# Hybrid decoder step: S5 tables by outer products, reversed S5 input at evacuation, first norm from token-major x, split weights kept as parts

## The chip, the cores and the metric

One Trainium2 chip, one of its cores. The metric is the device time of one execution of the program in microseconds (us). The engines have their own instruction queues, each worked off in order: TensorE (PE: matmuls; PEld: weight loads), VectorE (DVE), ScalarE (ACT), GpSimd (POOL) and SyncE (SP), which computes nothing and issues every DMA of this kernel.

## What is computed

One layer of a decoder trunk for 2048 prompt tokens and 8 sample tokens, width 1024, all in float32. Cut to its frame:

```python
z = rmsnorm(x, norm_mix) @ w_in                       # 2584 columns: mLSTM, S5 and gated-DeltaNet inputs
mix = concat([mlstm(z), s5(z) * glu, gated_delta_net(z)])
x = x + mix @ w_out
x = x + softmax(rmsnorm(x) @ w_mq @ mk.T / 16) @ mv @ w_mo    # 4 heads, 256 memory tokens
h = rmsnorm(x); x = x + (silu(h @ w_gate) * (h @ w_up)) @ w_down
y = rmsnorm(x)
```

S5 is a complex diagonal recurrence in 32 channel groups of 64 states: h[t] = lam * h[t-1] + B u[t], y[t] = Re(C h[t]) + d u[t]. The kernel runs it in chunks of 8 tokens, and for that needs tables made from lam: B times the powers 0 to 7 of lam, C times the powers 1 to 8, and the unit-size powers 0 to 128 of lam^8 (the array E).

## The kernel before

**Split matmuls.** Every float32 product is made of three fp32r matmuls. `gemm3` multiplies wh with xh, wh with xl and wl with xh: h is the value rounded to fp32r, l the rest. `split_x` and `hsplit` split activations (tiles H, ACT and DVE). Weights are split as they arrive, in `w_split_`: a DMA brings a raw tile wr of 128 x 1024 (512 KB), ACT rounds it to wh, and a subtraction gives wl:

```python
        S.copy(wh[:, 0:n], raw[:, 0:n])
        TT(V if i < 2 or i > 360 else G, wl[:, 0:n], raw[:, 0:n], wh[:, 0:n].bitcast(F32), SUB)
```

That is on GpSimd (G) for weights 2 to 360 of 512 and on VectorE (V) for the rest. wr, wh and wl have three buffers each. `load_w` runs two weights ahead with splits and up to three more with raw tiles. One weight serves 24 matmuls of 512 columns.

**Stages.** The prompt is cut into four segments of 512 tokens; the 8 sample tokens ride along. `win` does the input projection of a segment: 18 weights, one feature tile each, whose PSUM results (P) are scaled by the norm's row factors R and written out by DVE in `evac` (tile t), and then three token-major weights. The first `win` is interleaved with 16 tiles of memory keys and values (`mem_tile`), the next two with `fold` (products of those with attention weights). After the four `win` come four `post`, one for each segment, each over the same 95 weights: GLU, output projection, attention, FFN (22 gate, 22 up, 24 down); in segments 0 and 1 eight more for the sample tokens. So each of the 95 is fetched and split four times.

**Background work.** `s5_tables` (during the first `win`), `gdn`, `mlstm`, `s5` and the sample group's work are generators; `tick` moves them on by fixed rates between the weights' matmuls, and `drain` finishes what is left at fixed points (`s5_tables` after the first `win`). A scheduler then orders the instructions of each engine. `s5_tables` works with big tiles (three buffers, tag big), makes powers of lam by repeated complex products (`cmul`, six DVE instructions each), and writes tables to DRAM (T1, TB) from where transposes at L1166 and the S5 steps read them.

**First norm.** `win_sq` squares the feature-major x tiles on ACT and adds them up on DVE (`sq_acc`, tile acc); `norm_a` transposes acc on TensorE (L351) and reduces.

Of the kernel before, what the change touches and what calls it, by code (L numbers as in the profile page):

```python
# [66 lines left out]
def build(ctx, tc, I, O):  # L67
# [886 lines left out]
    def s5_tables():  # L954
        A0, A1 = Arena(), Arena()
        AB = Arena(bt())
        LN, RG = slice(0, 16), slice(16, 48)
# [107 lines left out]
        pb = [A0(bq), A0(bq)]  # L1065
        for q0 in (0, 8):
# [4 lines left out]
            Br = br[:, 0:1024].rearrange("p (q s c) -> p q s c", q=8, s=8)  # L1071
            Bi = bi[:, 0:1024].rearrange("p (q s c) -> p q s c", q=8, s=8)
            cmul(Br[:, :, 0, :], Bi[:, :, 0, :], bcq(cr, q0), bcq(ci, q0), pb[0], pb[1], tb[0], tb[1])
            for s_ in range(1, 8):
# [1159 lines left out]
```

## Time and profile before

| | |
|---|---|
| median of 3 runs | 3303.79 us (3300.41 to 3306.91) |
| the profiled execution, its own time | 3299.76 us, span 3298.0 us |
| TensorE busy | 3063.1 us, 93% of the span |
| VectorE busy | 2337.6 us, 71% |
| ScalarE, GpSimd busy | 1114.5 us (34%), 1103.8 us (33%) |
| DMA queue of SyncE | 448.43 MB, 45.7% of 16 engines' span |
| mean granted TensorE clock | 0.966 |

Times in the profile count from the start of the span. "Busy" is the time in which an engine executes; idle time before an instruction is put down to what ended it. The granted clock is 1 at TensorE's upper level and 0.5 at its lower. DMA share is the mean busy share of the 16 DMA engines. A helper's line stands for all its callers: L152 is any tensor-tensor instruction, L155 any scalar-tensor-tensor, L164 any matmul, so a tile's name tells which.

### The profile page before, as it was taken

The page shows a single profiled execution, that of the slowest core. Times are in us where ns is not written, and L with a number is a line of the kernel's source. Part 1 is how long each engine was busy: PE and PEld are TensorE (multiplying, and loading weights), DVE is VectorE, ACT ScalarE, POOL GpSimd, SP SyncE. Part 2 cuts the span into 40 slices and gives each one's busy share as a digit, 9 for nine tenths or more (in the row PEclk, how much of TensorE's full clock was granted, in tenths as well). Part 3 has the DMA queues.
Part 4 walks back from the last instruction along what each step waited for, and adds up shares of the span by engine and source line. Part 5 has one row for each costly group of instructions (what it writes and reads, how often), then busy time and mean ns, then how long its engine had stood idle before and what let it go on. Part 6 is the DMA issues. An engine that isn't in the chain of part 4 may idle for free.

```text
span 3298.0 us, 49267 instructions
## 1 busy us (share of the span) xinstructions
PE 3063.1 (93%) x18202; PEld 2619.2 (79%) x18202; DVE 2337.6 (71%) x4746; ACT 1114.5 (34%) x1882; POOL 1103.8 (33%) x706
## 2 busy tenths in 40 slices
PE   7777889999888998998999999989999999999998
PEld 6676678778877776787789999978777877888886
DVE  8783695786788689668886787687766767554445
ACT  3123433422542332234432322244324224332222
POOL 6332545534354444444544444344411000000000
PEclk9887999999999999999999999999999999999999
DMA  6679666666445345335443444352333325222332
GB/s 208 176 183 206 205 184 212 200 193 173 144 129 182 90 122 166 103 111 168 144 121 117 125 124 125 100 164 84 105 94 108 104 90 182 88 91 95 96 90 77
DMA packets 361361, 451.58 MB, mean 137 GB/s; under 512 B 144820, under 2 KB 246556, under 8 KB 361120
## 3 DMA queue, kind: packets, MB, share of 16 engines
q1 hardware_dynamic: 361120, 448.43, 45.7%
q8 instruction: 144, 2.36, 0.3%
q14 instruction: 97, 0.79, 0.1%
HBM read 378.73 MB, written 71.73 MB: 137 GB/s over the span
## 4 chain that ended last, share of the span: by engine, by line
PE 61%; DVE 13%; issue 3%; ACT 2%; DMA 2%; SPq 0%; POOL 0%; DVEq 0%; POOLq 0%; ACTq 0%
PE P L164 54%; PE M L164 5%; DVE t L155 3%; DVE big L152 3%; DVE x L152 1%; DVE s5h L155 1%; DVE TB L155 1%; DVE acc L152 1%; ACT wh L292 1%; DMA t<-mixd 1%; DVE x L155 1%; DVE H L152 0%; DVE H L155 0%; DMA x<-in_xT 0%; DMA ABd<-AW 0%
## 5 line engine op out<-in xcount | busy, mean ns | idle before, releaser
L164 PE MATMUL P<-H,wh 128*128 128x512 f32 (+2 forms) x8032 | 2190.0, 360 | 80.1 <-DVE t L152 32.7
L164 PEld LDWEIGHTS P<-H,wh 128*128 128x128 f32 x8032 | 1419.4, 191 | 309.4 <-issue 30.9
L164 PE MATMUL P<-H,wl 128*128 128x512 f32 (+2 forms) x4016 | 1430.8, 357 | 13.8 <-POOL wl L152 13.8
L152 POOL TENSOR_TENSOR wl<-wr,wh 128x1024 fp32r<-128x1024 f32 (+2 forms) x359 | 863.5, 2409 | 970.4 <-ACT wh L292 861.7
L292 ACT CAST wh<-wr 128x1024 fp32r<-128x1024 f32 (+3 forms) x512 | 521.1, 1020 | 1198.1 <-PE P L164 705.1
L164 PEld LDWEIGHTS P<-H,wl 128*128 128x128 f32 x4016 | 766.9, 191 | 124.6 <-POOL wl L152 16.3
L152 DVE TENSOR_TENSOR x<-x,P 128x512 f32<-128x512 f32 (+2 forms) x312 | 181.2, 587 | 141.9 <-PE P L164 128.9
L152 DVE TENSOR_TENSOR big<-big,big 32x87 f32<-32x87 f32 (+16 forms) x500 | 249.6, 499 | 18.7 <-DMA big<-ABd 10.8
L164 PE MATMUL P<-wh,H 128*128 128x256 f32 (+1 forms) x1280 | 244.6, 289 | 8.2 <-ACT pp L1717 6.3
L152 DVE TENSOR_TENSOR t<-P,R 128x512 f32<-128x512 f32 (+2 forms) x190 | 109.6, 581 | 165.7 <-PE P L164 142.0
L152 POOL TENSOR_TENSOR rs<-rcol,mhalf 128x4 f32<-128x4 f32 (+2 forms) x17 | 20.7, 1218 | 598.5 <-DVE rcol L161 598.2
L164 PEld LDWEIGHTS P<-wh,H 128*128 128x128 f32 x1280 | 204.7, 193 | 12.0 <-ACT pp L1717 8.2
L152 DVE TENSOR_TENSOR wl<-wr,wh 128x1024 fp32r<-128x1024 f32 (+1 forms) x153 | 183.8, 1202 | 25.5 <-ACT wh L292 22.8
L164 PE MATMUL P<-wl,H 128*128 128x256 f32 (+1 forms) x640 | 183.0, 287 | 0.5 <-POOL wl L152 0.5
L155 DVE SCALAR_TENSOR_TENSOR t<-P,R 128x512 f32<-128x512 f32 (+1 forms) x120 | 69.6, 583 | 153.9 <-PE P L164 152.2
L155 DVE SCALAR_TENSOR_TENSOR t<-t,t 128x512 f32<-128x512 f32 (+3 forms) x140 | 146.7, 1052 | 37.5 <-ACT t L1830 23.2
L152 DVE TENSOR_TENSOR H<-t,H 128x512 fp32r<-128x512 f32 (+1 forms) x120 | 123.5, 1037 | 46.3 <-ACT H L1600 46.2
L164 PEld LDWEIGHTS P<-wl,H 128*128 128x128 f32 x640 | 123.6, 193 | 1.2 <-POOL wl L152 0.7
L1600 ACT CAST H<-t 128x512 fp32r<-128x512 f32 (+1 forms) x120 | 73.5, 621 | 141.7 <-DVE t L152 124.8
L155 DVE SCALAR_TENSOR_TENSOR t<-g,VEC,t 128x256 f32<-128x256 f32 x144 | 99.5, 691 | 20.0 <-ACT t L724 18.4
L155 DVE SCALAR_TENSOR_TENSOR H<-x,VEC,H 128x512 fp32r<-128x512 f32 (+2 forms) x104 | 102.2, 996 | 8.5 <-ACT H L334 6.6
L152 DVE TENSOR_TENSOR acc<-acc,t 128x512 f32<-128x512 f32 (+1 forms) x115 | 99.1, 861 | 9.2 <-ACT t L343 7.3
(414 smaller groups left out, 3114.7 us busy)
## 6 DMA issues: line engine op xcount, KB each, us to landing
wr<-in_wgate SPq DMA_DIRECT2D x88, 512.0 KB
...
```

Source lines behind the costliest of these rows:

```text
L152: eng.tensor_tensor(out=out, in0=a, in1=b, op=op)
L155: V.scalar_tensor_tensor(out=out, in0=a, scalar=s, in1=b, op0=op0, op1=op1, **kw)
L164: PE.matmul(out, l, r, start=st, stop=sp)
L292: S.copy(wh[:, 0:n], raw[:, 0:n])
L1600: S.copy(h[:, 0:T], src[:, 0:T])
```

## The change

Four edits in one:

1. **S5 tables.** The powers 0 to 8 of lam are made once (pw, in tile s5h), and B and C are multiplied with them as outer products, six DVE instructions of 1024 elements each time instead of eight complex products of 128. E is doubled up to power 16 and completed by one outer product of its first 16 powers with the powers 16 to 112.
2. **S5 input.** The four S5 feature tiles are written reversed and regrouped by the evacuation itself; the copy to a second tile (zu) goes. Sample columns are evacuated straight into ZS. In `s5`, two 128 x 1 copies for each group go from DVE to ACT.
3. **First norm.** `win_sq` loads x a second time, token-major (xtok, 8 tiles of 256 KB for a segment), and ACT squares and sums each row. The adds on DVE and the transposes of acc on TensorE go for the four input norms.
4. **Weights behind the mixers.** In `post` of segment 0 each of the 95 weights is split as before, and wh and wl are stored to DRAM (two DMAs). In segments 1 to 3 they are loaded from there into wh and wl (two DMAs in place of one), without a raw tile and without a split. 285 weights lose their split: 249 casts of 1024 columns and 36 of 768 on ACT, 151 subtractions on DVE, 134 on GpSimd. `load_w` keeps its look-ahead of two weights.

```diff
     def w_split_():
         i = wst["s"]
-        n = WL[i][1]
-        raw = raws.pop(i)
+        src, n, key, mode = WL[i]
         wh = wp.tile([128, WN], F32R, name=nm("wh"), tag="wh", bufs=3)
         wl = wp.tile([128, WN], F32R, name=nm("wl"), tag="wl", bufs=3)
-        S.copy(wh[:, 0:n], raw[:, 0:n])
-        TT(V if i < 2 or i > 360 else G, wl[:, 0:n], raw[:, 0:n], wh[:, 0:n].bitcast(F32), SUB)
+        if mode == "pre":
+            for q, t in enumerate((wh, wl)):
+                SY.dma_start(t[:, 0:n].bitcast(F32), wsd(key, n)[q])
+        else:
+            raw = raws.pop(i)
+            S.copy(wh[:, 0:n], raw[:, 0:n])
+            TT(V if i < 2 else G, wl[:, 0:n], raw[:, 0:n], wh[:, 0:n].bitcast(F32), SUB)
+            if mode == "store":
+                for q, t in enumerate((wh, wl)):
+                    SY.dma_start(wsd(key, n)[q], t[:, 0:n].bitcast(F32))
         splits[i] = (wh, wl)
         wst["s"] += 1
+
+    WSD = {}
+
...
 
     def win_sq(s):
         p = pre[s.i]
-        p["acc"] = acct()
-        for k in range(KD):
-            sq_acc(p["acc"], p["x"][k], p["T"], k == 0)
+        col = mt([128, 8], "rcol", 3)
+        if s.sa:
+            V.memset(col, 1.0)
+        for j in range(s.n + s.sa):
+            m = 128 if j < s.n else NB
+            for hh in range(2):
+                q = tt()
+                SY.dma_start(q[0:m, 0:512], I["xtok"][s.x0 + j * 128:s.x0 + j * 128 + m, hh * 512:hh * 512 + 512])
+                S.activation(q[0:m, 0:512], q[0:m, 0:512], AF.Square, accum_out=p["sq"][0:m, 2 * j + hh:2 * j + hh + 1])
+        p["col"] = col
 
     def win_rs(s):
-        pre[s.i]["rs"] = norm_a(pre[s.i]["acc"], s.n, s.sa)
+        p = pre[s.i]
+        col, n = p["col"], s.n + s.sa
+        sq3 = p["sq"].rearrange("p (j a) -> p j a", a=2)
+        V.tensor_reduce(out=col[:, 0:s.n], in_=sq3[:, 0:s.n, :], axis=AX.X, op=ADD)
+        if s.sa:
+            V.tensor_reduce(out=col[0:NB, s.n:n], in_=sq3[0:NB, s.n:n, :], axis=AX.X, op=ADD)
+        TS(V, col[:, 0:n], col[:, 0:n], 1.0 / D, MUL, EPS, ADD)
+        p["rs"] = mt([128, 8], "rs", 3)
+        rsq(p["rs"][:, 0:n], col[:, 0:n], n)
 
...
         def evac(n, Ps):
             R = st["R"]
             z = tt()
+
+            def zt(a, m):
+                if n < 14:
+                    return z[:, a:a + m]
+                return z[:, 0:512].rearrange("p (s c) -> p c s", s=8)[:, a // 8:(a + m) // 8, ::-1]
+
+            def vw(x):
+                return x if n < 14 else x.rearrange("p (c s) -> p c s", s=8)
+
             for P, b0, bn in Ps:
+                m = min(bn, s.np - b0)
                 if n < 2:
-                    STT(z[:, b0:b0 + bn], P[:, 0:bn], 0.125, R[:, b0:b0 + bn], MUL, MUL)
+                    STT(zt(b0, m), vw(P[:, 0:m]), 0.125, vw(R[:, b0:b0 + m]), MUL, MUL)
                 else:
-                    TT(V, z[:, b0:b0 + bn], P[:, 0:bn], R[:, b0:b0 + bn], MUL)
+                    TT(V, zt(b0, m), vw(P[:, 0:m]), vw(R[:, b0:b0 + m]), MUL)
+                if m < bn:
+                    STT(ZS[:, n, :], P[:, m:bn], 0.125 if n < 2 else 1.0, R[:, s.np:T], MUL, MUL)
             if n < 14:
                 SY.dma_start(zf[n, :, s.tok0:s.tok0 + s.np], z[:, 0:s.np])
             else:
-                zu = tt()
-                V.tensor_copy(zu[:, 0:512].rearrange("p (s c) -> p c s", s=8)[:, :, ::-1],
-                              z[:, 0:512].rearrange("p (c s) -> p c s", s=8))
                 f0 = (n - 14) * 128
                 SY.dma_start(uf[s.i // 2, f0:f0 + 128, :, (s.i % 2) * 64:(s.i % 2) * 64 + 64],
-                             zu[:, 0:512].rearrange("p (s c) -> p s c", s=8))
-            if s.sa:
-                V.tensor_copy(ZS[:, n, :], z[:, s.np:T])
+                             z[:, 0:512].rearrange("p (s c) -> p s c", s=8))
 
         pend = []
         for n in range(18):
...
 
         tb = [A1(bq), A1(bq)]
         pb = [A0(bq), A0(bq)]
...
+        def outer(orr, oi, x, q0, s0):
+            def v(t):
+                return t[:, 0:1024].rearrange("p (q s c) -> p q s c", q=8, s=8)
+
+            def xv(k):
+                return x[k].unsqueeze(2).to_broadcast([128, 8, 8, 16])
+
+            def pv(k):
+                return bc(pw[k][:, q0:q0 + 8, s0:s0 + 8], 16)
+
+            tm = bt()
+            TT(V, v(orr), pv(0), xv(0), MUL)
+            TT(V, v(tm), pv(1), xv(1), MUL)
+            TT(V, orr[:, 0:1024], orr[:, 0:1024], tm[:, 0:1024], SUB)
+            yield
+            TT(V, v(oi), pv(0), xv(1), MUL)
+            TT(V, v(tm), pv(1), xv(0), MUL)
+            TT(V, oi[:, 0:1024], oi[:, 0:1024], tm[:, 0:1024], ADD)
+            yield
+
         for q0 in (0, 8):
             SY.dma_start(pb[0], I["s5b"][:, 0, q0:q0 + 8, :])
             SY.dma_start(pb[1], I["s5b"][:, 1, q0:q0 + 8, :])
...
-                yield
+            cmul(bb_[0], bb_[1], bcq(cr, q0), bcq(ci, q0), pb[0], pb[1], tb[0], tb[1])
+            yield
+            yield from outer(br, bi, bb_, q0, 0)
             for g2_ in range(2):
                 q = slice(64 * g2_, 64 * g2_ + 64)
...
-            pr_, pi_ = pb
-            for s_ in range(8):
-                cmul(Br[:, :, s_, :], Bi[:, :, s_, :], pr_, pi_, bcq(lr, q0), bcq(li, q0), tb[0], tb[1])
-                pr_, pi_ = Br[:, :, s_, :], Bi[:, :, s_, :]
-                yield
+            yield from outer(br, bi, pb, q0, 1)
             TS(V, bi[:, 0:1024], bi[:, 0:1024], -1.0, MUL)
             ng = bt()
             TS(V, ng[:, 0:1024], br[:, 0:1024], -1.0, MUL)
...
-            while m < 128:
+            while m < 16:
                 x1 = tt()[:, 0:8 * m].rearrange("p (q c) -> p q c", q=8)
                 x2 = tt()[:, 0:8 * m].rearrange("p (q c) -> p q c", q=8)
                 cmul(Er[:, :, m + 1:2 * m + 1], Ei[:, :, m + 1:2 * m + 1], Er[:, :, 1:m + 1], Ei[:, :, 1:m + 1],
...
+                     hi_[1][:, :, a0 - 1:a0].to_broadcast([128, 8, an]), x1, x2)
+            yield
+            E4 = [x[:, :, 17:129].rearrange("p q (a b) -> p q a b", a=7) for x in (Er, Ei)]
+            n4 = n2[:, 0:896].rearrange("p (q a b) -> p q a b", q=8, a=7)
+            LO = [x[:, :, 1:17].unsqueeze(2).to_broadcast([128, 8, 7, 16]) for x in (Er, Ei)]
+            HI = [bc(x, 16) for x in hi_]
+            TT(V, E4[0], LO[0], HI[0], MUL)
+            TT(V, n4, LO[1], HI[1], MUL)
+            TT(V, E4[0], E4[0], n4, SUB)
+            yield
+            TT(V, E4[1], LO[0], HI[1], MUL)
+            TT(V, n4, LO[1], HI[0], MUL)
+            TT(V, E4[1], E4[1], n4, ADD)
+            yield
             TT(V, n2[:, 0:1032], er[:, 0:1032], er[:, 0:1032], MUL)
             for hh in range(2):
...
-            V.tensor_copy(gs[:, 0:1], Hend[:, g:g + 1])
+            S.copy(gs[:, 0:1], Hend[:, g:g + 1])
             V.tensor_tensor_scan(out=gs[:, 1:129], data0=rhoC[:, g:g + 1].to_broadcast([128, 128]), data1=x1,
                                  initial=Hend[:, g:g + 1], op0=MUL, op1=ADD)
-            V.tensor_copy(Gend[:, g:g + 1], gs[:, 128:129])
+            S.copy(Gend[:, g:g + 1], gs[:, 128:129])
             mc = mt([128, 136], "mc")
             ms = mt([128, 128], "ms", 2)
...
@@ -1562,37 +1648,37 @@
 
 
     def wl_post(seg):
+        mode = "store" if seg == 0 else "pre"
         for n in range(2):
-            plain(I["wglu"][n])
+            plain(I["wglu"][n], key=("u", n), mode=mode)
         for n in range(8):
-            plain(I["wout"][n])
-
+            plain(I["wout"][n], key=("o", n), mode=mode)
         for h in range(4):
             for i in range(2):
...
                 if f != f0 or ci == 0:
-                    plain(I["wgate"][f])
-                plain(I["wup"][f])
+                    plain(I["wgate"][f], key=("g", f), mode=mode)
+                plain(I["wup"][f], key=("p", f), mode=mode)
             if ci + 1 < len(FCH):
-                plain(I["wgate"][f0 + fn])
+                plain(I["wgate"][f0 + fn], key=("g", f0 + fn), mode=mode)
```

What the change moves, at three places of the engines' orders. Numbers behind names count buffers.

TensorE, the transposes of T1 in `s5_tables` (line L1166 before, L1252 after; t is the tile they transpose, big the C operand beside them). Before, they stand behind all matmuls of the first `win`, behind the first ones of the second `win` (P of 512 columns):
```order
L164 MATMUL P_3022<-H_2765,wh_2926 128x512
L164 MATMUL P_3022<-H_2764,wl_2927 128x512
L164 MATMUL M_2680<-big_2620,t_2623 128x16
L1166 MATMUL M_2680<-C,t_2623 128x128
L164 MATMUL M_2680<-big_2620,t_2623 128x16
L164 MATMUL M_2688<-big_2620,t_2623 128x16
L1166 MATMUL M_2688<-C,t_2623 128x128
L164 MATMUL M_2688<-big_2620,t_2623 128x16
```
After, the same ones stand within the first `win`, whose feature tiles come in two P tiles of 264 and 256 columns; this is behind feature tile 15 of 0 to 17:
```order
L164 MATMUL P_2441<-H_316,wh_2183 128x256
L164 MATMUL P_2441<-H_315,wl_2184 128x256
L164 MATMUL M_2094<-big_2054,t_2057 128x16
L1252 MATMUL M_2094<-C,t_2057 128x128
L164 MATMUL M_2094<-big_2054,t_2057 128x16
L164 MATMUL M_2102<-big_2054,t_2057 128x16
L1252 MATMUL M_2102<-C,t_2057 128x128
L164 MATMUL M_2102<-big_2054,t_2057 128x16
```
The 32 transposes and the 64 small matmuls beside them now stand in runs behind feature tile 15, behind the last memory tile and within feature tile 16; tile 17 and the token-major weights come after them.

SyncE, at the first gate weights of segment 2 (wr a raw weight tile, Bd and ws_B the folded output weights, ws_g and ws_p the parts of the gate and up weights; XBd, XC, XT belong to `gdn`). Before:
```order
L307 DMA wr_23951<-Bd 128x1024
L307 DMA wr_23998<-in_wgate 128x1024
L856 DMA XBd<-big_23663 32x1024
L307 DMA wr_24054<-in_wup 128x1024
L862 DMA XC<-XBd 32x8x32
L857 DMA XBd<-big_23666 32x1024
L862 DMA XC<-XBd 32x8x32 x3
```
After:
```order
L295 DMA wh_23886<-ws_B_10504 128x1024
L295 DMA wl_23887<-ws_B_10504 128x1024
L894 DMA XBd<-big_23563 32x1024
L895 DMA XBd<-big_23566 32x1024
L295 DMA wh_23940<-ws_B_10553 128x1024
L295 DMA wl_23941<-ws_B_10553 128x1024
L900 DMA XC<-XBd 32x8x32 x4
L900 DMA XT<-XBd 32x8x32 x4
L295 DMA wh_23981<-ws_g_10605 128x1024
L295 DMA wl_23982<-ws_g_10605 128x1024
L295 DMA wh_24050<-ws_p_10683 128x1024
```
Each weight now has two DMAs of 512 KB, which go straight into wh and wl and so wait for the matmuls of the weight three places earlier; the gdn work's DMAs stand between them in the one queue, as before.

VectorE, the C tables of the first eight lam rows within the first `win` (t and M, P are evacuations). Before, in pieces of 128 elements (`big<-TB` and `TB<-big,TB` alternate, six to a complex product):
```order
L152 TENSOR_TENSOR TB_282<-big_868,TB_281 128x128
L152 TENSOR_TENSOR TB_282<-big_869,TB_281 128x128
L152 TENSOR_TENSOR big_869<-TB_282 128x8x16
L152 TENSOR_TENSOR TB_282<-big_868,TB_281 128x128
L152 TENSOR_TENSOR TB_282<-big_869,TB_281 128x128
L152 TENSOR_TENSOR t_1198<-M_1173,s_385 128x256
L152 TENSOR_TENSOR big_868<-TB_282 128x8x16
L152 TENSOR_TENSOR TB_282<-big_868,TB_281 128x128
L152 TENSOR_TENSOR TB_282<-big_869,TB_281 128x128
L152 TENSOR_TENSOR big_869<-TB_282 128x8x16
```
After, in pieces of 1024:
```order
L152 TENSOR_TENSOR big_791<-s5h_285,TB_282 128x1024
L152 TENSOR_TENSOR TB_282<-TB_282 128x16
L152 TENSOR_TENSOR big_793<-s5h_285,TB_282 128x1024
L152 TENSOR_TENSOR t_828<-M_803,s_387 128x256
L161 TENSOR_SCALAR TB_282<-TB_282 128x16
L152 TENSOR_TENSOR big_792<-s5h_285,TB_282 128x1024
L152 TENSOR_TENSOR big_791<-big_791,big_793 128x1024
L152 TENSOR_TENSOR TB_282<-TB_282 128x16 x2
L152 TENSOR_TENSOR t_898<-P_846,R_514 128x264
```
An evacuation stands behind one or two pieces of 1024 elements, where it stood behind some nine of 128.

## Rows read from the trace of the kernel before

**Rows 1.** The page: span, TensorE's busy time, the chain by engine
```profile
span 3298.0 us, 49267 instructions
...
PE 3063.1 (93%) x18202; PEld 2619.2 (79%) x18202; DVE 2337.6 (71%) x4746; ACT 1114.5 (34%) x1882; POOL 1103.8 (33%) x706
...
PE 61%; DVE 13%; issue 3%; ACT 2%; DMA 2%; SPq 0%; POOL 0%; DVEq 0%; POOLq 0%; ACTq 0%
```

**Rows 2.** Windows by stage: busy us, granted clock, DMA share, GB/s
```profile
core 0: us, PE busy (x) PEld busy (x) DVE busy (x) ACT busy (x) POOL busy (x), PEclk, DMA share, GB/s
0.00:264.00 264.00, 195.64 (x1412) 187.57 (x1412) 213.86 (x534) 69.93 (x97) 119.63 (x59) 0.90 0.66 187
264.00:330.00 66.00, 48.80 (x251) 42.71 (x252) 13.13 (x47) 23.61 (x68) 12.44 (x6) 0.74 0.98 220
330.00:846.00 516.00, 477.51 (x2726) 391.98 (x2725) 373.15 (x954) 186.06 (x342) 244.00 (x201) 0.96 0.66 195
846.00:1480.00 634.00, 587.96 (x3270) 486.19 (x3270) 490.29 (x927) 216.29 (x371) 281.77 (x153) 0.96 0.42 129
1480.00:2090.00 610.00, 584.76 (x4478) 542.26 (x4477) 489.49 (x1027) 215.92 (x379) 280.23 (x178) 0.98 0.43 129
2090.00:2740.00 650.00, 629.30 (x3539) 524.10 (x3538) 449.70 (x838) 226.07 (x380) 160.46 (x106) 0.99 0.36 107
2740.00:3298.00 558.00, 539.17 (x2535) 444.36 (x2533) 308.00 (x423) 176.58 (x249) 5.31 (x4) 0.99 0.32 102
```

**Rows 3.** Waits of TensorE, 0 to 264 us: total us, times, longest
```profile
PE P L164 <- DVE t L152: 34.5, 7, 15.4
...
PE M L351 <- DVE acc L152: 4.6, 2, 3.9
```

**Rows 4.** Waits of VectorE, 0 to 264 us
```profile
DVE big L1111 <- DMA TB<-big: 12.1, 2, 9.5
DVE big L152 <- DMA TB<-big: 12.0, 1, 12.0
```

**Rows 5.** Waits of TensorE, 264 to 330 us
```profile
PE M L1166 <- DMA t<-T: 11.3, 3, 7.3
```

**Rows 6.** VectorE groups, 0 to 420 us: count, busy us, mean ns, idle
```profile
L152 DVE TENSOR_TENSOR TB<-big,TB 128x128 f32<-128x128 f32 x112 | 35.9, 362 | 1.2
L152 DVE TENSOR_TENSOR big<-TB 128x128 f32<-128x128 f32 x64 | 31.1, 486 | 17.6 <-DMA TB<-big 12.0 <-DMA T<-big 4.5
...
L152 DVE TENSOR_TENSOR big<-big,big 128x1032 f32<-128x1032 f32 x4 | 4.8, 1230 | 0.0
```

**Rows 7.** The page's groups: split and norm adds on VectorE
```profile
L152 DVE TENSOR_TENSOR wl<-wr,wh 128x1024 fp32r<-128x1024 f32 (+1 forms) x153 | 183.8, 1202 | 25.5 <-ACT wh L292 22.8
...
L152 DVE TENSOR_TENSOR acc<-acc,t 128x512 f32<-128x512 f32 (+1 forms) x115 | 99.1, 861 | 9.2 <-ACT t L343 7.3
```

**Rows 8.** Windows of segment 0 behind the mixers, columns as in rows 2
```profile
1000.00:1100.00 100.00, 92.66 (x468) 73.09 (x467) 81.92 (x214) 33.69 (x49) 45.13 (x21) 0.97 0.57 177
```

**Rows 9.** Waits of TensorE, 1480 to 3298 us
```profile
PE P L164 <- DVE x L152: 11.8, 6, 4.7
PE M L748 <- DVE t L155: 9.4, 2, 5.7
PE M L743 <- ACT t L735: 8.5, 6, 2.9
```

**Rows 10.** VectorE's groups by form, 1560 to 2170 us
```profile
L152 DVE TENSOR_TENSOR H<-t,H 128x520 fp32r<-128x520 f32 x22 | 35.6, 1617 | 12.4 <-ACT H L1600 12.3
```

**Rows 11.** VectorE's groups by form, 2900 to 3270 us
```profile
L152 DVE TENSOR_TENSOR H<-t,H 128x512 fp32r<-128x512 f32 x22 | 15.1, 686 | 3.4 <-ACT H L1600 3.4
```

**Rows 12.** The chain that ended last: start us, length us, what
```profile
939.48 3.60 DMA wr<-in_wmq
...
2929.16 348.90 PE P L164 x1503
```

**Rows 13.** Waits of SyncE's queue, 1480 to 3298 us
```profile
SPq L1262 <- DVE big L152: 14.0, 2, 10.2
```

More of the change, by code (lines that the diff above doesn't have):

```diff
@@ L279, in w_raw_ @@
         i = wst["r"]
-        src, n = WL[i]
+        wst["r"] += 1
+        src, n, key, mode = WL[i]
+        if mode == "pre":
+            return
         raw = wp.tile([128, WN], F32, name=nm("wr"), tag="wr", bufs=3)
@@ L283, in w_raw_, with wsd @@
         raws[i] = raw
-        wst["r"] += 1
     def w_split_():
         i = wst["s"]
-        n = WL[i][1]
-        raw = raws.pop(i)
+        src, n, key, mode = WL[i]
         wh = wp.tile([128, WN], F32R, name=nm("wh"), tag="wh", bufs=3)
         wl = wp.tile([128, WN], F32R, name=nm("wl"), tag="wl", bufs=3)
-        S.copy(wh[:, 0:n], raw[:, 0:n])
-        TT(V if i < 2 or i > 360 else G, wl[:, 0:n], raw[:, 0:n], wh[:, 0:n].bitcast(F32), SUB)
+        if mode == "pre":
+            for q, t in enumerate((wh, wl)):
[7 more added lines that the diff above has]
+                    SY.dma_start(wsd(key, n)[q], t[:, 0:n].bitcast(F32))
         splits[i] = (wh, wl)
         wst["s"] += 1
+    WSD = {}
+    def wsd(key, n):
+        if key not in WSD:
+            WSD[key] = dtile([2, 128, n], "ws_" + "_".join(str(q) for q in key))
+        return WSD[key]
     def load_w():
@@ L304, in load_w, with plain @@
         return splits.pop(i)
-    def plain(src, n=1024):
-        WL.append((lambda raw: SY.dma_start(raw[:, 0:n], src), n))
+    def plain(src, n=1024, key=None, mode="raw"):
+        WL.append((lambda raw: SY.dma_start(raw[:, 0:n], src), n, key, mode))
     def gemm3(P, n, W, wofs, X, b0, bn, ks, mid=None, m=128, first=True, last=True):
@@ L392, in win_load @@
         T = s.np + (NB if s.sa else 0)
-        p = {"x": [], "X": {}, "T": T}
+        p = {"x": [], "X": {}, "T": T, "sq": mt([128, 10], "rsq", 2)}
         for k in range(KD):
@@ L956, in s5_tables @@
         AB = Arena(bt())
+        A2 = Arena(mt([128, 2, 256], "s5h", 1).rearrange("p a b -> p (a b)"))
         LN, RG = slice(0, 16), slice(16, 48)
@@ L1065, in s5_tables @@
         pb = [A0(bq), A0(bq)]
+        bb_ = [A1(bq), A1(bq)]
+        pw = [A2([128, 16, 9]) for _ in range(2)]
+        V.memset(pw[0][:, :, 0:1], 1.0)
+        V.memset(pw[1][:, :, 0:1], 0.0)
+        V.tensor_copy(pw[0][:, :, 1:2], lr.unsqueeze(2))
+        V.tensor_copy(pw[1][:, :, 1:2], li.unsqueeze(2))
+        m = 1
+        while m < 8:
+            w1 = A1([128, 16, 4], "w1")[:, :, 0:m]
+            w2 = A1([128, 16, 4], "w2")[:, :, 0:m]
+            cmul(pw[0][:, :, m + 1:2 * m + 1], pw[1][:, :, m + 1:2 * m + 1], pw[0][:, :, 1:m + 1], pw[1][:, :, 1:m + 1],
+                 pw[0][:, :, m:m + 1].to_broadcast([128, 16, m]), pw[1][:, :, m:m + 1].to_broadcast([128, 16, m]), w1, w2)
+            m *= 2
+        yield
[15 more added lines that the diff above has]
+            yield
         for q0 in (0, 8):
@@ L1070, in s5_tables @@
             br, bi = bt(), bt()
[L1071 to L1074, printed above, removed]
-                cmul(Br[:, :, s_, :], Bi[:, :, s_, :], Br[:, :, s_ - 1, :], Bi[:, :, s_ - 1, :],
-                     bcq(lr, q0), bcq(li, q0), tb[0], tb[1])
-                yield
+            cmul(bb_[0], bb_[1], bcq(cr, q0), bcq(ci, q0), pb[0], pb[1], tb[0], tb[1])
+            yield
+            yield from outer(br, bi, bb_, q0, 0)
             for g2_ in range(2):
@@ L2103, in _prep @@
     r["xT"] = np.concatenate([xp[:, 0:512], xs, xp[:, 512:]], axis=1)
+    r["xtok"] = np.ascontiguousarray(r["xT"].T)
     r["memT"] = A["mem_prompt"][0].T
```

21 lines of the change are left out of this document (14 added, 7 removed).

## The prediction, made blind

> **What bounds the kernel now.** First the page: TensorE is busy 93% of the span and makes 61% of the chain that ended last [rows 1]. Late in the run, where nothing disturbs it, 1503 matmuls take 348.90 us, 0.232 us each [rows 12]; at that pace a weight's 24 matmuls last 5.57 us. Removing work from the other engines thus gains only where TensorE waits for them, and the next view says where that is. By stages [rows 2] TensorE is idle 264 - 195.6 = 68.4 us in the first `win`, 17.2 us in the 66 us behind it, 38.5 us in the other three, and 46.0, 25.2, 20.7 and 18.8 us in the four `post`. The granted clock adds a little: it is below 1 on average wherever TensorE waits, 0.74 in the worst stage. So the change can win at most some 235 us of idle time, and only 65 of it lies where the weights come ready split.
>
> The waits say who is late in the first `win`: evacuations, 34.5 us [rows 3]. They are late because VectorE itself, in order, stands before a big tile whose table is still being written to DRAM: 12.1 and 12.0 us [rows 4]. In the 66 us after it TensorE works off table transposes, waiting 11.3 us for the reloads of T1 [rows 5], at 0.74 of the clock and with the DMA engines 98% busy [rows 2].
>
> **Edit 1, S5 tables.** Removed are the complex products of 128 elements, 112 + 64 instructions, 35.9 + 31.1 = 67 us of VectorE [rows 6]. Added are 24 instructions of 1024, nearest to the one of 1032 at 1.230 us, so 29.5 us, and some 35 small ones for the powers and the new first products, at 0.2 to 0.36 us about 9 us. E changes the number of elements little. VectorE saves about 28 us. But of the 34.5 us at least 24 come from DMA, and the buffers' chain (write a table, wait, write the next) is kept; so I credit 4 us of TensorE time to it.
>
> The larger part is the place. The generator has fewer steps, and the transposes now stand within the first `win`. The 66 us stage holds 48.8 us of TensorE work at 0.74 of the clock, about 48.8 x 0.76 = 37 us at the full one (an estimate), so up to 29 us of it can go. Within the `win` the transposes still come in runs on an engine that works in order, and each run waits for its reload: I leave the 11.3 us in. That gives -18 us. Bounds: 0, if the whole chain now stops the `win` it is in, and -29 - 17 = -46 us, if half of the evacuations' waits go as well.
>
> **Edit 3, first norm.** The transpose of acc waited 4.6 us [rows 3]; 28 adds of 0.861 us go [rows 7], 24 us of VectorE over four segments. -4 us in the first `win`. Against this, x is loaded twice: 2.1 MB a segment, at about 310 GB/s (129 GB/s at a share of 0.42 [rows 2]) 7 us of all DMA engines. Five of the first eight loads stand ahead of weights that the start waits for, 1.3 MB, 4 us: +3 us, bounds 0 and +7. Edits 1 and 3 together: -4 - 18 - 4 + 3 = -23 us.
>
> **Edit 2, and the rest of stages two to four.** Copies and adds that go are some 30 us of 373 us VectorE work in the stage from 330 to 846 us. TensorE is idle there 38.5 us, not only for VectorE: a tenth of it, -4 us; bounds -12 and +4 (the 128 x 1 copies now need ACT, and a DVE instruction waits for them).
>
> **Edit 4, segment 0 behind the mixers.** The splits stay; 95 weights gain 1 MB of stores each, 83 x 1.05 + 12 x 0.79 = 96 MB in 634 us, 152 GB/s. At 310 GB/s for a full share that is 0.49. The stage has 0.42 [rows 2], together 0.91; in the two stretches with much loading it has 0.57 and about as much [rows 8], together 1.06. There the DMA engines would be 6 us late in each 100 us. Raw tiles are loaded up to five weights, 28 us, ahead, and cover most of it; a stored pair keeps its buffer until it is out, but that buffer is not needed again for two weights, 11 us. I take +6 us; bounds 0 and +30 (all of the mixers' DMA round trips become longer in a queue that is 0.91 full).
>
> The Trainium skill ("DMA: Bandwidth & Descriptors", Specifications) gives about 358 GB/s as HBM's limit for one core. By that figure the worst stretch, 177 + 152 = 329 GB/s, would still fit, and this term would be 0. The row decides against it here: that stretch has 177 GB/s at a share of 0.57, where many packets are small.
>
> **Edit 4, segments 1 to 3.** 151 subtractions on VectorE go, nearly all of 183.8 us [rows 7], 134 on GpSimd, and 285 casts on ACT. Waits that this shortens are those for VectorE and ACT, 11.8 + 9.4 + 8.5 = 29.7 us [rows 9], at the passages between segments. I credit a quarter and the clock that comes back with it: -8 us, bounds 0 and -25. In segment 1 VectorE gains without losing an instruction: its subtraction H of 520 columns takes 1617 ns while GpSimd splits [rows 10], and 686 ns for 512 where GpSimd is idle [rows 11].
>
> The Trainium skill ("SBUF — State Buffer", Who interferes with whom) says that a VectorE instruction with two SBUF inputs and a GpSimd instruction that reads SBUF lock each other out for a whole instruction. The rows agree. By that rule segment 1 gives back more than I credit, which is the first rival below.
>
> What the loads cost is the other side. A raw tile was fetched early; a pair can only start when the weight three places earlier is done, 2 x 5.57 = 11.1 us before it is needed. A 512 KB load takes 3.60 us [rows 12], the second half behind it 1.7 us at 310 GB/s, and issue some 0.5 us: 5.8 us, so 5 us are spare. In the one queue other DMAs stand between, and those wait too: up to 10.2 us for a gyd store [rows 13]. Such a wait over 5 us delays the pair behind it. I count some ten of them and 1 us lost on average: +8 us; bounds 0 and +60.
>
> **The sum.** -23 - 4 + 6 - 8 + 8 = -21 us from the profiled execution's own 3299.8 us, 3279 us. That execution lies 4 us below the median of the runs shown; adding that, 3283 us. I give 3282.
>
> **Rivals.**
> - *More is freed than I credit.* The first `win` loses half its evacuation waits (-46 in place of -18 - 4), VectorE without GpSimd's lock meets segment 1 and the passages early (-25 in place of -8), and the pairs are always in time (0 in place of +8): 3282 - 24 - 17 - 8 = 3233 us. For it: the 1617 against 686 ns, and DMA shares of 0.43, 0.36 and 0.32 in these segments, to which some 0.5 for the pairs is added at most. Against it: TensorE loses only 65 us there altogether.
> - *The table chain moves and nothing is gained.* The transposes stop TensorE within the `win` for as long as they did behind it: 3282 + 18 = 3300 us, no change. For it: their chain is one of DMA round trips, none of which the change removes, and the edit puts them ahead of work that could have run.
> - *Pairs arrive late.* In segments 1 to 3 TensorE waits for wh or wl at the start of weights, because the queue is held by a mixer's DMA and only two weights of look-ahead are left. 285 pairs at 0.25 us on average cost 71 us, with 8 already counted: 3282 + 63 = 3345 us. It decides from 0.13 us per pair on: 21 + 8 = 29, plus the 6.6 us of 0.2%, over 285. For it: the queue's waits of up to 10 us against 5 us spare. Against it: a wait at the queue was as long before, at the same places, and the queue mostly waits for weights.
>
> **How the numbers follow.** 0.2% (6.6 us) is what runs of this kernel can tell from no change: faster is below 3297.2 us, slower above 3310.4. The forecast has a chance of 0.43 and reaches from 3262 to 3297; more freed 0.19; the table chain moves 0.14, of which a little falls below 3297; late pairs, or segment 0 bound by DMA at its +30, 0.24. Faster is 0.43 + 0.19 + 0.02 = 0.64, same 0.12, slower 0.24. The range leaves out a tenth at either end: from just below the first rival, 3228, to between the second and the last, 3335.
>
> **What would show it.** Right: transposes of `s5_tables` before 264 us with TensorE back at full clock by 300 us; the first stretch up to the fourth `win`'s end some 27 us shorter; `post` of segment 0 longer by under 10 us with a DMA share near 0.9; H subtractions of some 0.7 us in segment 1; waits of TensorE on wh and wl that sum to under 15 us. Wrong: waits on DMA wh<-ws or wl<-ws among TensorE's largest, a granted clock below 0.98 in segments 1 to 3, or a first `win` that grows by as much as the 66 us behind it shrink.

## The result and the profile after

After takes 3246.62 us (median of 4 runs, 3243.17 to 3248.63), before 3303.10 (4 runs) on the same chip: a ratio of 0.983, 95% interval 0.9817 to 0.9843. That is 56.5 us less where the prediction had 22. The time lies in the stated range (3228 to 3335), but not in the forecast case (3262 to 3297), and the working behind that case did not hold.

The page of after; the rows answer to [rows 1]:

```profile
span 3244.8 us, 49242 instructions
...
PE 3049.1 (94%) x18185; PEld 2612.5 (81%) x18185; DVE 1942.0 (60%) x4305; ACT 866.8 (27%) x1761; POOL 776.7 (24%) x572
```

VectorE lost 396 us of work, GpSimd 327, ScalarE 248, and the span only 53. Where those 53 lie, the windows of after by stage tell (columns as in [rows 2]). Their bounds are the points at which as much of the split weights' matmuls is done as at 317, 846, 1480, 2090 and 2740 us of before; TensorE's counts agree within 3 matmuls, apart from the first stage, where the norm's ten transposes are gone.

```profile
0.00:317.00 317.00, 231.76 (x1587) 222.55 (x1588) 202.27 (x418) 90.45 (x178) 129.21 (x62) 0.85 0.78 215
317.00:839.00 522.00, 487.08 (x2790) 400.65 (x2788) 353.99 (x892) 205.00 (x433) 246.53 (x204) 0.97 0.69 204
839.00:1464.00 625.00, 585.17 (x3267) 483.67 (x3268) 491.79 (x924) 215.54 (x369) 280.91 (x153) 0.97 0.80 280
1464.00:2058.00 594.00, 580.72 (x4476) 540.54 (x4475) 365.23 (x966) 146.80 (x355) 75.04 (x94) 0.99 0.61 205
2058.00:2684.00 626.00, 623.64 (x3540) 520.08 (x3539) 325.86 (x782) 126.67 (x277) 40.54 (x56) 1.00 0.57 195
2684.00:3244.80 560.80, 540.70 (x2533) 444.96 (x2531) 202.90 (x326) 82.30 (x152) 4.50 (x4) 0.99 0.53 191
```

Two windows of before that were not shown:

```profile
0.00:317.00 317.00, 231.43 (x1599) 219.55 (x1600) 226.04 (x577) 91.52 (x164) 127.35 (x62) 0.87 0.71 193
2090.00:2330.00 240.00, 219.30 (x1454) 196.84 (x1453) 180.09 (x327) 97.17 (x178) 101.93 (x58) 0.97 0.37 117
```

The stages' lengths, before and after: 317 and 317; 529 and 522; 634 and 625; 610 and 594; 650 and 626; 558 and 561 us. The first stage, to which the prediction gave most (23 us), gave nothing between these two traces. The three segments with ready pairs, which it had at 0, gave 37: there TensorE's idle time fell from 64.8 to 35.7 us and its busy time from 1753.2 to 1745.1, beside a granted clock of 0.99, 1.00 and 0.99 where it was 0.98, 0.99 and 0.99. Segment 2 won its 24 us in its first part, between 2090 and 2330 us of before:

```profile
2058.00:2273.00 215.00, 212.64 (x1452) 192.09 (x1451) 134.56 (x336) 63.39 (x141) 15.15 (x20) 1.00 0.64 217
```

TensorE's waits in segments 1 to 3 of after (as [rows 9]):

```profile
PE P L164 <- ACT pp L1803: 4.7, 6, 0.8
PE P L164 <- DMA wh<-ws_A: 4.6, 3, 2.1
PE P L164 <- DMA wh<-ws_B: 3.7, 3, 2.0
PE M L367 <- DVE acc L152: 2.7, 1, 2.7
PE M L385 <- POOL rs L152: 2.2, 1, 2.2
PE P L164 <- DMA wh<-ws_o: 1.9, 1, 1.9
PE M L164 <- DVE mR L152: 1.8, 1, 1.8
PE P L164 <- DVE x L152: 1.5, 2, 1.1
PE P L164 <- DMA wl<-ws_A: 1.2, 1, 1.2
PE P L164 <- DMA wl<-ws_o: 1.1, 2, 0.8
PE P L164 <- DMA wl<-ws_B: 0.5, 1, 0.5
```

Of the waits for VectorE and ScalarE of [rows 9], 29.7 us, only 1.5 are left. The other rows of that view of before, 25.4 us in sum, are 11.4 here, and the pairs, new, come late for 13.0 us. Together that is the 29 us by which the idle time fell. VectorE's groups by form, 1500 to 2100 us, show the H subtraction at 697 ns where [rows 10] had 1617:

```profile
L152 DVE TENSOR_TENSOR x<-x,P 128x264 f32<-128x264 f32 x40 | 16.9, 423 | 12.1 <-PE P L164 11.5
...
L152 DVE TENSOR_TENSOR H<-t,H 128x520 fp32r<-128x520 f32 x21 | 14.6, 697 | 9.6 <-ACT H L1686 9.5
...
L152 DVE TENSOR_TENSOR mc<-gs,TB 128x128 f32<-128x128 f32 x31 | 9.7, 313 | 0.3
```

In the first stage VectorE still stands, in order, before DMA of the table chain, and TensorE waits for the evacuations nearly as long as before (33.0 us, 34.5 in [rows 3]). VectorE's waits in after, 0 to 317 us (as [rows 4]), TensorE's wait for the evacuations, the matmuls and transposes that read the reloaded t, and TensorE in the 63 us in which they lie:

```profile
DVE big L152 <- DMA big<-in_s5d: 15.7, 1, 15.7
...
DVE big L152 <- DMA TB<-big: 11.2, 1, 11.2
```

```profile
PE P L164 <- DVE t L152: 33.0, 6, 9.5
```

```profile
L1252 PE MATMUL M<-C,t x32: 270/450/472, 210.2 to 270.7; 128*128 128x128 f32 x32
...
  DMA t<-T: 10.7, 2
  DVE big L159: 10.7, 1
```

```profile
202.00:265.00 63.00, 34.45 (x206) 33.73 (x206) 21.81 (x32) 18.88 (x59) 9.91 (x5) 0.66 0.85 220
```

The transposes came into the `win`, as the prediction said, and brought their hole with them: 63 us at a granted clock of 0.66 with 28.6 us idle, where before had 66 us at 0.74 [rows 2].

### The profile page after: what moved, and what is told of

It is laid out like the page before. It is cut to its first block, busy times and chain, and to the rows that moved or that the text cites. A ratio compares the mean times of both kernels' runs of the same rounds, so it can differ in the third digit from the quotient of the medians.

```text
span 3244.8 us, 49242 instructions
## 1 busy us (share of the span) xinstructions
PE 3049.1 (94%) x18185; PEld 2612.5 (81%) x18185; DVE 1942.0 (60%) x4305; ACT 866.8 (27%) x1761; POOL 776.7 (24%) x572
## 4 chain that ended last, share of the span: by engine, by line
PE 65%; DVE 7%; DMA 4%; issue 2%; ACT 1%; POOL 1%; SPq 0%; POOLq 0%; DVEq 0%; ACTq 0%
PE P L164 59%; PE M L164 5%; DVE big L152 2%; DVE t L155 1%; DVE s5h L155 1%; DMA t<-mixd 1%; DVE x L152 0%; POOL wl L152 0%; DVE H L155 0%; DMA wh<-ws_B 0%; DMA wl<-ws_o 0%; DVE acc L152 0%; DVE t L152 0%; DMA ABd<-AW 0%; DMA t<-in_xtok 0%
## 5 line engine op out<-in xcount | busy, mean ns | idle before, releaser
L152 POOL TENSOR_TENSOR wl<-wr,wh 128x1024 fp32r<-128x1024 f32 (+3 forms) x225 | 543.5, 2419 | 625.6 <-ACT wh L298 540.7
L298 ACT CAST wh<-wr 128x1024 fp32r<-128x1024 f32 (+3 forms) x227 | 231.3, 1021 | 400.4 <-PE P L164 220.9
L152 DVE TENSOR_TENSOR big<-big,big 32x60 f32<-32x60 f32 (+16 forms) x512 | 236.3, 462 | 31.3 <-DMA big<-ABd 21.9
L152 DVE TENSOR_TENSOR t<-P,R 128x512 f32<-128x512 f32 (+3 forms) x190 | 115.7, 614 | 214.5 <-PE P L164 184.0
L155 DVE SCALAR_TENSOR_TENSOR t<-t,t 128x512 f32<-128x512 f32 (+3 forms) x140 | 106.7, 767 | 63.4 <-ACT t L1916 42.3
L152 DVE TENSOR_TENSOR H<-t,H 128x512 fp32r<-128x512 f32 (+1 forms) x120 | 89.0, 748 | 66.4 <-ACT H L1686 66.0
L1916 ACT ACTIVATE t<-t 128x512 f32<-128x512 f32 (+1 forms) x88 | 55.7, 633 | 261.2 <-DVE t L152 260.9
L152 POOL TENSOR_TENSOR ms<-gs,TB 128x128 f32<-128x128 f32 x64 | 32.4, 507 | 362.3 <-ACT Gend L1320 120.9
L155 DVE SCALAR_TENSOR_TENSOR H<-x,VEC,H 128x512 fp32r<-128x512 f32 (+2 forms) x104 | 89.8, 879 | 34.6 <-ACT H L350 32.5
L350 ACT ACTIVATE H<-x,VEC 128x512 fp32r<-128x512 f32 (+1 forms) x96 | 67.3, 719 | 90.3 <-DVE x L152 57.8
```

The costliest lines, as they stand in the source:

```text
L152: eng.tensor_tensor(out=out, in0=a, in1=b, op=op)
L155: V.scalar_tensor_tensor(out=out, in0=a, scalar=s, in1=b, op0=op0, op1=op1, **kw)
L350: S.activation(h[:, 0:T], x[:, 0:T], AF.Copy, scale=scale)
L1916: S.activation(th[:, 0:Tb], gt[:, 0:Tb], AF.Tanh, scale=0.5)
```

## The experiments

Theory A: each edit acts in its own stage, and behind the mixers it is edit 4. Theory B: the gain behind the mixers needs the other edits. Theory C: edit 1 gained its 22 us, and edit 3 lost as much. Within A, **G** says that GpSimd's splits held VectorE up, **V** that VectorE's own splits did. The chips of the experiments run the kernel before in 3312 to 3314 us, not 3303, so all are compared by the ratio to the kernel before on their own chip; 0.001 is 3.3 us. Where an expectation gives a time, the ratio times 3303.1 us is the measured one to hold against it. Between traces of different chips the first two stages differ: 317 and 522 us in after, 324 and 527 in after_2; from segment 0 on the two agree within some 2 us a stage. Intervals are 95%.

**Which edit.** Kernels put together from the hunks of the diff:

```
w_only     before + edit 4 (w_raw_, w_split_, wsd, plain, wl_post)
no_w       after  - edit 4
no_tables  after  - edit 1 (s5_tables)
no_norm    after  - edit 3 (win_load, win_sq, win_rs, xtok)
tab_only   before + edit 1
```

*w_only.* 

> The kernel before with edit 4 alone (weights behind the mixers split once, kept as parts). Theory A, each edit acts in its own stage: between before and after the passage through segments 1 to 3 became 37 us shorter and segment 0 behind the mixers 10 us, so edit 4 alone gives 3303 - 37 = 3266 us, or 3256 if the 10 us of segment 0 are its own as well. Theory B, the gain behind the mixers needs the relief of VectorE by the other edits: 3280 us or more.

*no_w.* 

> The kernel after without edit 4 (only edits 1 to 3 and the two copies on ScalarE). Theory A: the first 846 us lost 7 us and nothing else moves: 3296 us, or 3286 if the 10 us of segment 0 come from these edits. Theory B (they work behind the mixers too): 3275 us or less.

*no_tables.* 

> The kernel after without edit 1 (S5 tables as before, the other edits stay). Theory A, the table chain moved into the first win and gains nothing there: within 6 us of after, 3241 to 3253, with the transposes again behind the first win at half clock and the point at which they end at about 317 us. Theory C, edit 1 gained what was forecast (22 us) and edit 3 lost as much by its loads at the start: 3262 us or more.

*no_norm.* 

> The kernel after without edit 3 (first norm from squares of x with adds on VectorE, no token-major x). Theory A, edit 3 is worth a few us at most: 3247 to 3252. Theory C, its loads and its ScalarE work in the first win cost what edit 1 gained: 3229 us or less, with the transposes' end before 300 us.

*tab_only.* 

> The kernel before with edit 1 alone (S5 tables by outer products, the transposes move into the first win). The prediction gave it 22 us, 0.993. If the chain of table, DMA and reload only moves, as in the rival: 0.998 to 1.0. If edit 3 hides what edit 1 gains (no_norm against w_only: 0.980 against 0.986): 0.994 to 0.996.

*after_2*, after itself again. 

> The kernel after once more, beside the kernel before on the chip of the next three, as their yardstick. Expected: a ratio of 0.983 within 0.002.

| | ratio | interval | at 3303.1, us |
|---|---|---|---|
| w_only | 0.9862 | 0.9848 to 0.9875 | 3258 |
| no_w | 0.9976 | 0.9967 to 0.9986 | 3295 |
| no_tables | 0.9852 | 0.9835 to 0.9869 | 3254 |
| no_norm | 0.9800 | 0.9787 to 0.9813 | 3237 |
| tab_only | 0.9972 | 0.9961 to 0.9983 | 3294 |
| after_2 | 0.9840 | 0.9827 to 0.9854 | 3250 |

Edit 4 alone is worth 46 us, edits 1 to 3 alone 8; together 54 of the 56 measured, so A holds and B falls. Edit 1 alone gives 9 us, not 22, between the two values that were expected; without it after loses 4 to 7 us (0.9852), at the edge of A's 6 and far from C's 3262. Without edit 3 after is 10 to 13 us faster (0.980 against 0.983 and 0.984), so edit 3 took back half or more of what edits 1 and 2 gained beside edit 4 (0.980 against 0.9862, 20 us).

Part of this shows at the start. The first stage, up to the work that before has done at 317 us, of before_V1 (described below; up to here it is the kernel before), no_w, no_norm and tab_only:

```profile
0.00:327.00 327.00, 234.70 (x1596) 222.60 (x1597) 227.79 (x577) 91.07 (x162) 125.89 (x62) 0.84 0.72 187
0.00:325.00 325.00, 228.17 (x1592) 219.18 (x1593) 202.91 (x418) 90.10 (x178) 129.00 (x62) 0.85 0.81 209
0.00:319.00 319.00, 231.17 (x1596) 221.47 (x1597) 207.42 (x442) 90.18 (x163) 128.59 (x61) 0.86 0.79 196
0.00:320.00 320.00, 228.53 (x1595) 218.67 (x1596) 211.58 (x452) 90.20 (x161) 126.55 (x61) 0.87 0.78 196
```

With tables and norm as before it takes 327 us; with edits 1 to 3 325 (324 to 327 in after_2, put_G, put_V and no_stores); without edit 3 319; with edit 1 alone 320. So, by one trace each, edit 1 wins some 7 us here, and edit 3 takes 5 to 8 of them back. That is theory C in its form, with 7 to 9 us in place of 22. TensorE's waits for GpSimd (tiles wl and rs) are 16.4 us in this stage of no_w and 6.4 in that of no_norm; whether they are what edit 3 costs was not tested.

**GpSimd or VectorE.** The first two kernels put back into after one engine's share of the work, with a result that nothing uses; the third moves GpSimd's share in before.

```diff
 put_G, put_V: after, w_split_, mode "pre", behind the two loads
+            if i <= 360:                       # put_V: if i > 360
+                dmy = wp.tile([128, WN], F32, name=nm("wr"), tag="wr", bufs=3)
+                TT(G, dmy[:, 0:n], wh[:, 0:n].bitcast(F32), wl[:, 0:n].bitcast(F32), SUB)   # put_V: TT(V, ...
 before_V1: before, w_split_
-        TT(V if i < 2 or i > 360 else G, wl[:, 0:n], raw[:, 0:n], wh[:, 0:n].bitcast(F32), SUB)
+        TT(V if i < 2 or i > 218 else G, wl[:, 0:n], raw[:, 0:n], wh[:, 0:n].bitcast(F32), SUB)
```

*put_G.* 

> The kernel after, with a subtraction of GpSimd for each ready pair of the weights 219 to 360, where GpSimd split them before (its result is used nowhere). Theory G, in segments 1 and 2 it was GpSimd's reading of SBUF that made VectorE late: VectorE's H subtractions of segment 1 are back at about 1.6 us, and 25 to 40 us of the 37 us won behind segment 0 come back, 3270 to 3287 us. Theory V, VectorE's own 151 subtractions were it: within 5 us of after.

*put_V.* 

> The kernel after, with a subtraction of VectorE for each ready pair from weight 361 on, where VectorE split them before (its result is used nowhere). Theory V, VectorE's own subtractions were what TensorE waited for: 15 to 37 us come back, 3262 us or more. Theory G: at most 5 us, 3242 to 3252.

*before_V1.* 

> The kernel before, with the splits of the weights 219 to 360 on VectorE instead of GpSimd, and nothing else changed. Theory G, it was GpSimd's reading of SBUF in segments 1 and 2 that cost the time, whoever does the splits: some 25 to 40 us are won without keeping any parts, a ratio of 0.988 to 0.992, and VectorE's H subtractions of segment 1 fall to about 0.7 us. Theory V, what matters is how much work VectorE has: it gains 142 instructions of 1.2 us, 170 us, and the time stays or grows, a ratio of 0.998 or more.

Measured: put_G 0.9953 (0.9941 to 0.9966), put_V 0.9842 (0.9829 to 0.9856), before_V1 0.9899 (0.9884 to 0.9914). GpSimd's 134 added subtractions give 37 us back; VectorE's 151, which stand where before had them, from the later part of segment 2 on, give back nothing; and before with GpSimd's splits of segments 1 and 2 on VectorE wins 33 us with no parts kept. Windows of segment 1 and of the first part of segment 2, of put_G:

```profile
1475.00:2088.00 613.00, 588.15 (x4478) 544.84 (x4477) 470.65 (x965) 144.47 (x353) 283.04 (x178) 0.98 0.60 199
2088.00:2323.00 235.00, 218.82 (x1449) 195.53 (x1448) 172.74 (x324) 63.07 (x141) 100.89 (x57) 0.98 0.59 197
```

And of before_V1:

```profile
1499.00:2087.00 588.00, 578.93 (x4477) 538.97 (x4476) 454.91 (x1119) 216.80 (x378) 62.14 (x86) 0.99 0.46 134
2087.00:2312.00 225.00, 216.44 (x1448) 195.50 (x1447) 165.48 (x355) 96.87 (x177) 15.56 (x20) 0.97 0.40 124
```

In segment 1 of put_G VectorE runs the same instructions as in after (965 and 966) and is busy 470.7 us instead of 365.2. In before_V1 it runs 92 more than in before (1119 and 1027 [rows 2]) and is busy 35 us *less*. VectorE's groups by form, put_G first:

```profile
L152 DVE TENSOR_TENSOR mc<-gs,TB 128x128 f32<-128x128 f32 x31 | 20.9, 673 | 0.4
L152 DVE TENSOR_TENSOR H<-t,H 128x520 fp32r<-128x520 f32 x19 | 16.9, 892 | 7.2 <-ACT H L1689 7.1
...
L152 DVE TENSOR_TENSOR x<-x,P 128x264 f32<-128x264 f32 x32 | 13.4, 420 | 7.4 <-PE P L164 7.2
```

```profile
L152 DVE TENSOR_TENSOR wl<-wr,wh 128x1024 fp32r<-128x1024 f32 x86 | 107.4, 1249 | 13.3 <-ACT wh L292 12.7
...
L152 DVE TENSOR_TENSOR H<-t,H 128x520 fp32r<-128x520 f32 x19 | 13.2, 692 | 2.1 <-ACT H L1600 2.0
```

Which instruction is hit differs: H takes 892 ns in put_G, not the expected 1.6 us, and 1617 in before; mc takes 673 in put_G and 313 in after. The addition x<-x,P, whose second input is in PSUM, takes 420 ns beside GpSimd and 423 without. The Trainium skill ("SBUF — State Buffer", Who interferes with whom) says that a VectorE instruction with at most one SBUF input, outside the modes that use both of VectorE's ports, does not contend with GpSimd, and one with two does with a GpSimd instruction that reads SBUF; these rows agree on both.

The added subtractions also read the pairs, and so could hold their buffers. That is not what costs the time: TensorE's waits for pairs in the two stretches sum to 5.4 us in put_G and 10.7 in after. What came back are waits for VectorE (put_G, 1475 to 2323 us):

```profile
PE M L789 <- DVE t L155: 10.4, 4, 4.7
PE P L164 <- DVE x L152: 7.4, 8, 2.1
```

**Stores and late pairs.**

```diff
 no_stores: after; also wsd gives one tensor for each n
-            if mode == "store":
+            if mode == "store" and n not in WSD:
 ring9: after; raw, wh and wl take the one tag "w9" with bufs=9
-        while wst["s"] <= i + 2 and wst["s"] < len(WL):
+        while wst["s"] < len(WL) and wst["s"] <= i + (3 if WL[wst["s"]][3] == "pre" else 2):
```

*no_stores.* 

> The kernel after without the stores of segment 0 but the first of each size; every pair of segments 1 to 3 is loaded from one of these few tensors, so it leaves out 90 MB of stores, and the products of those segments are of wrong weights. If the stores cost what the prediction gave them (6 us, up to 30), the stretch behind the mixers in segment 0 becomes 6 us or more shorter and the ratio 0.982 or less. If the DMA engines carry them beside the work, the stretch stays within 2 us of after's 625 us and the ratio at 0.984.

*ring9.* 

> The kernel after, with the nine buffers of wr, wh and wl as one ring and ready pairs loaded three weights ahead instead of two. If the waits of TensorE on the pairs (13 us in the trace of after, 0.1 to 2.1 us each) come from the look-ahead, they fall to under 3 us and the time falls by 8 to 15 us, with the clock that comes back: 3232 to 3239. If they come from the queue being held by the DMAs of mixers, which stand ahead of the loads however early these are asked for, they stay, and so does the time (within 4 us of after).

Measured: no_stores 0.9846 (0.9825 to 0.9867), ring9 0.9808 (0.9792 to 0.9824). Without the stores no gain can be seen, though the intervals leave room for some 6 us: the DMA share of segment 0 falls from 0.80 to 0.44, and the segment is 633 us long instead of 625, with the next one 587 instead of 594. Windows of no_stores:

```profile
850.00:1483.00 633.00, 588.09 (x3266) 485.36 (x3266) 492.12 (x926) 215.48 (x368) 280.78 (x153) 0.96 0.44 130
1483.00:2070.00 587.00, 579.70 (x4475) 540.10 (x4475) 364.64 (x965) 147.00 (x356) 76.57 (x94) 0.99 0.62 206
```

Together the two segments last 1219 us in after, 1220 in no_stores and 1244 in before. So after's 9 us of segment 0 look like no gain of that segment alone: some 8 us stand on the one or on the other side of its end. In sum these 9 and the 37 behind them are w_only's 46 us. In ring9 TensorE's waits for pairs fall from 13.0 us to 2.3, two rows; the time falls by 10 us, as expected.

```profile
PE P L164 <- DMA wl<-ws_A: 1.2, 1, 1.2
PE P L164 <- DMA wh<-ws_A: 1.1, 1, 1.1
```

**No split on GpSimd.** What G asks for next:

```diff
 ring_V0: ring9             ("i < 2 or i > 115" on VectorE: segment 0 too)
 before_Vall: before        ring_Vall: ring9        ring_Vall_nn: ring9 - edit 3
 after_Vall: after          w_Vall: w_only          ring_no_norm: ring9 - edit 3, splits as in ring9
+        TT(V, wl[:, 0:n], raw[:, 0:n], wh[:, 0:n].bitcast(F32), SUB)     # all that end in Vall, and Vall_nn
```

*ring_no_norm.* 

> The ring of nine buffers with pairs three weights ahead, and without edit 3 (first norm as before). If edit 3 costs time in the first 846 us (no_norm had a ratio of 0.980 against 0.983 and 0.984 of after), it is 0.978 and beats both kernels; if that difference was one of chips, 0.981, the ring's own.

*ring_V0.* 

> The ring of nine buffers, and the splits of segment 0 behind the mixers (103 weights) on VectorE instead of GpSimd too. Theory G: VectorE's other work there runs without GpSimd's lock, and what it saves pays for the splits; the 40 us of TensorE's waits in this segment fall by 10 or more, a ratio of 0.978 or less. Rival: VectorE is already 79 percent busy there, and 103 subtractions of 1.2 us make it late at the S5 and mLSTM steps; a ratio of 0.982 or more.

*before_Vall.* 

> The kernel before with every split on VectorE, in the wins and segment 0 too, and nothing else changed. Theory G: what ring_V0 won in segment 0 (some 40 us) and before_V1 in segments 1 and 2 (33 us) come together without any of the four edits, a ratio of 0.976 to 0.98; and if TensorE's waits for evacuations in the first win (33 us) are GpSimd's too, 0.972 or less. Rival: in the first win VectorE is held by DMA round trips of the S5 tables, as the prediction said; the wins gain nothing or lose by 116 more subtractions, 0.98 or more.

*ring_Vall.* 

> ring_V0 with the splits of the wins (weights 2 to 115) on VectorE as well. Theory G for the wins: their end comes 10 to 30 us earlier than in ring_V0, a ratio of 0.959 to 0.965. Rival (DMA round trips and VectorE's own work hold the wins): 0.968 or more, with the waits of TensorE on DVE t in the first 317 us unchanged at some 33 us.

*ring_Vall_nn.* 

> ring_Vall without edit 3 (first norm as before). If edit 3 costs 10 us (0.9763 without against 0.9808 with it in the ring), its ratio is 0.003 below ring_Vall's. If it only seemed to cost them because GpSimd made the start tight, both are within 0.0015.

*after_Vall.* 

> The kernel after with every split that is left on VectorE, and the buffers as in after. before_Vall has 0.9635 and ring_Vall 0.9541: if the ring's earlier loads are worth their 10 us here too, 0.957; if the pairs come in time once VectorE is early, 0.954.

*w_Vall.* 

> The kernel before with edit 4 and every split that is left on VectorE, without edits 1 to 3. If what the change won behind the mixers came only from GpSimd's splits leaving, kept parts give nothing beside before_Vall: 0.962 to 0.965. If the subtractions and casts that they take from VectorE and ScalarE count too, 0.960 or less.

| | ratio | interval | median, us |
|---|---|---|---|
| ring_no_norm | 0.9763 | 0.9747 to 0.9779 | 3236.63 |
| ring_V0 | 0.9678 | 0.9662 to 0.9693 | 3206.71 |
| before_Vall | 0.9635 | 0.9621 to 0.9648 | 3191.18 |
| w_Vall | 0.9600 | 0.9581 to 0.9619 | 3181.05 |
| after_Vall | 0.9548 | 0.9533 to 0.9563 | 3162.65 |
| ring_Vall | 0.9541 | 0.9528 to 0.9554 | 3160.76 |
| ring_Vall_nn | 0.9542 | 0.9529 to 0.9555 | 3161.43 |

The one line of before_Vall wins 121 us, more than twice what the whole change does. TensorE's own waits for GpSimd's splits are a small part of it, 13.8 us before its wl matmuls by the page of before. The page of before_Vall, and its windows for the work that before does in 317 us and in its segment 0:

```profile
PE 3024.9 (95%) x18202; PEld 2599.4 (82%) x18202; DVE 2220.3 (70%) x5105; ACT 1119.0 (35%) x1882; POOL 255.8 (8%) x347
```

```profile
0.00:291.50 291.50, 221.54 (x1597) 212.11 (x1598) 206.06 (x618) 91.52 (x162) 26.67 (x21) 0.88 0.80 210
...
806.00:1402.00 596.00, 577.01 (x3269) 480.34 (x3269) 448.56 (x1026) 218.81 (x372) 42.65 (x54) 0.99 0.46 135
```

VectorE runs 359 instructions more than in before and is busy 117 us less [rows 1]; segment 0 falls from 634 to 596 us, the first stage from 317 to 291.5 (327 in before_V1). One half of the rival in before_Vall's expectation holds there: TensorE's waits for the evacuations stay, next to the DMA of the tables:

```profile
PE P L164 <- DVE t L152: 31.2, 4, 19.4
```

Edit 4 in itself is worth 12 us beside it (0.9600 against 0.9635), edits 1 to 3 another 17 (0.9548). The ring's earlier loads, worth 10 us before, and edit 3, which cost as much, make no difference that can be told here (0.9541, 0.9542 and after_Vall's 0.9548); all three are faster than both kernels.

## Why the prediction was wrong

**The step that failed most: "Edit 4, segments 1 to 3 ... I credit a quarter", -8 us, bounds 0 and -25.** Measured: 37 us net of the late pairs, some 50 without them. The step asked which of TensorE's waits named VectorE or ScalarE, found 29.7 us, and placed them "at the passages between segments". The waits' names were right, their cause was one engine further back: [rows 10] and [rows 11] showed GpSimd making VectorE late, but the prediction kept that out of the sum, left it to a rival, and gave it no price of its own. Put_G gives it: 134 GpSimd subtractions cost 37 us; before_V1: the same splits on VectorE cost less than on GpSimd, by 33 us. The bound of 25 was wrong too: the three rows alone fell by 28 us, and 14 us of smaller rows and 8 us of TensorE's busy time went with them.

**"+8 for late pairs"** was right in mechanism and near in size: 13.0 us of waits, 10 us by ring9. The sign of being wrong, waits on wh<-ws among TensorE's largest, came all the same, because the larger ones had gone. The rival "Pairs arrive late" does not hold: 0.05 us for each of 285 pairs, not the 0.13 from which it decides.

**"Edits 1 and 3 together: -23 us."** This failed too: nothing by 317 us. The VectorE relief is there (202 against 226 us busy), and TensorE's waits for the evacuations stayed, as the step itself had warned. "So up to 29 us of it can go" is the part that failed (its 0.76 stands for a granted 0.74, which would make it 30): the transposes moved, the reloads' 10.7 us moved with them, with another 10.7 us for CC, whose sign VectorE turns (the TS behind `bload(0)`) only after its own waits for DMA, and so did the low clock (0.66). This is nearly the rival "The table chain moves and nothing is gained", true of its stage, though not of the whole: edit 1 alone gives 9 us, 7 of them in this stage. Edit 3's "-4 +3" was mis-sized: it costs 10 to 13 us while GpSimd splits, 5 to 8 of them in the first stage, and nothing that can be told when VectorE does. Which of its loads, squares on ScalarE or places in the order costs this was not taken apart.

**"Edit 2, and the rest of stages two to four, -4"**: 7 us shorter, within its bounds of -12 and +4, with edits 1 and 3 in the same stage.

**"Edit 4, segment 0 behind the mixers", +6**: no cost to be seen (no_stores), its lower bound, with some 6 us of room in the intervals. The load was forecast nearly right, 0.80 of the DMA engines against 0.91, at 280 GB/s, and hidden. By the figure that the prediction cites from the Trainium skill ("DMA: Bandwidth & Descriptors", Specifications) this term is 0, and the runs do not contradict it.

**The sum by stages**, forecast and measured: first stage -23 and 0; wins -4 and -7; segment 0 +6 and -9; segments 1 to 3 0 and -37. That the total still fell in the range is in part luck: the first stage's 23 us too many hide more than half of the 37 too few; had they come, 3223 us would have been below the range. The rival "More is freed than I credit" (3233) names the lock, the early passages and 0 for the pairs; its first term did not come, its second was twice as large (some 50 us for 25), its third was 13 us, and the time lies between it and the forecast.
